# Constant rows at another place, a final norm on VectorE, scratch in a PSUM bank, a priority for SSD

## The chip, the cores and the metric

The kernel runs on one core of a Trainium2 chip. The core has five engines that each work through their own list of instructions in order: TensorE (PE, matmuls), VectorE (DVE), ScalarE (ACT), GpSimd (POOL) and SyncE (SP, which here only issues transfers). TensorE writes to PSUM, a small memory of eight banks per core, and everything else lives in SBUF or in DRAM. The metric is the time of one execution on the device in microseconds, smaller being better; the median of several runs counts.

## The reference

One layer of a hybrid diffusion transformer with 2048 latent tokens and 256 context tokens, width 1024. Three groups of heads share one input projection: pooling, a bidirectional state-space scan (SSD) and a bidirectional gated delta rule (GDN). Then come an output projection, a mixture of 16 experts in which each expert chooses 256 tokens, and a last RMSNorm.

```python
def rms_norm(x, g):
    x32 = x.astype(F32)
    y = x32 * lax.rsqrt(jnp.mean(x32 * x32, axis=-1, keepdims=True) + EPS) * g.astype(F32)
    return y.astype(x.dtype)
...
def gdn_chunked(q, k, v, g, beta, s0):
...
    xm = jnp.where(strict, jnp.einsum('bnhik,bnhjk->bnhij', kb, kc) * decay, 0.0)
    eye = jnp.eye(CHUNK, dtype=xm.dtype)
    tm = lax.linalg.triangular_solve(xm + eye, jnp.broadcast_to(eye, xm.shape), left_side=True, lower=True,
                                     unit_diagonal=True)
    u = jnp.einsum('bnhij,bnhjv->bnhiv', tm, vc * bc[..., None])
    w = jnp.einsum('bnhij,bnhjk->bnhik', tm, kb * jnp.exp(gc)[..., None])
...
def ssd_chunked(xdt, log_a, bm, cm, s0):
...
    states = jnp.einsum('bchjs,bchjp->bchsp', bc * jnp.exp(ac[..., -1:] - ac)[..., None], xc)
    chunk_decay = jnp.exp(ac[..., -1])

    def step(s, inp):
        st, dc = inp
        return s * dc[..., None, None] + st, s
```

The triangular solve is what the inverse in the kernel computes, and the last `rms_norm` is the final norm.

## The kernel before

Precise float32 products are made of three faster ones: a helper `mm3` (lines 133 to 135) multiplies high by high, low by high and high by low parts, and `split` (lines 192 and 193) makes the parts, the high one as a rounded copy on ScalarE and the low one as a difference on VectorE. The program is traced in the order of the code, and a scheduler then puts each engine's instructions into one static order by priorities, which follow the code except where a block asks for a higher one (`tc.high_priority`). Each engine works through its own list and never overtakes.

**Start (0 to 173 us).** SyncE's queue loads the modulation weights (`aw` from `ada_w`), the context and latent rows `xt`, and two slices of the input weights whose products `dt`, `ab` and `z` are needed first. Line 295 rounds such a slice to `wzh`, line 296 makes `wzl`. `raw_T` transposes the normed rows into `raw` (lines 240 to 245), `modulate` scales them (line 350) and splits them into `hTh` and `hTl`, `t1_ctx` (line 371 copies its result into a buffer) and `t1` multiply. Between them lines 334 to 343 write constant rows (ones and minus ones that later scans read as parts of larger rows) into `gpq_d` and `fsr_d` in DRAM, from buffers of `zrow()`: a pool of two buffers named `zt` which also hold the scratch of line 230, the copy of line 371 and the results of `t1`.

**Projection and convolutions (173 to 660 us)** and some preparation (to 780 us) are not touched.

**Scans (780 to 1450 us).** GDN needs for each chunk the inverse of a unit lower triangular matrix. `gdn_inv` does this by columns on blocks of 32: `column(c)` multiplies an outer product into a scratch tile (line 1071) and subtracts it (line 1073), 31 columns for each block, on VectorE. The GDN chain itself goes step by step: line 1163 updates the state `gS` of each direction from a matmul in PSUM, line 1135 makes `gR`, lines 1183 to 1190 the output `oe`, which goes to DRAM as `go_d`. The SSD scan goes tile by tile beside it (`ssd_f`, and the output in lines 892 to 932). In the scans, the eight PSUM banks are `pp` (2), `ps` (3, constant NPS), `pm`, `pc` and `po`. A plan in code hands out pieces of inverse, SSD and preparation per step; GDN's preparation asks for priority HPP, the chain for HPO.

**Output projection and router (1450 to 1710 us).** Line 1390 brings `go` back and transposes it, line 1437 takes the projection's results out of PSUM.

**Experts (1710 to 2374 us).** For each of 16 experts: `slots` compares (`oh`, line 1605) and gathers rows, `up` and `down` multiply, `weights` loads a piece `wr` of 128x1024, rounds it (line 1644) and makes its low part `wl` (line 1647) on VectorE. Line 1672 multiplies the gate's result `sg` once per expert. `down` scatters into `x_d`. From expert 9 the final norm runs beside the experts, as a list of tasks of which `up` takes one at each piece of weights: `norm_all` norms all 16 tiles, and `norm_rows(q)` norms again the rows that expert q changed later. `norm_scale` computes a reciprocal root by Newton steps of small operations on VectorE (lines 109 to 120, helper `rsqrt_bits`, tiles `fr1t` and `fr1y` on one column, `fr2t` and `fr2y` on two), scales the tile on ScalarE (line 1693) and multiplies with `fg` on GpSimd (line 1694). The last three experts write their rows directly, in one product on VectorE (line 1691).

## Time and profile before

| | |
|---|---|
| median of 3 runs | 2382.78 us (2379.66 to 2393.21) |
| the profiled execution, its own time | 2376.19 us |
| span in its profile | 2374.4 us |
| busy: TensorE, VectorE, ScalarE, GpSimd | 2078.8, 1734.5, 1077.7, 826.5 us |
| transferred | 424.72 MB, mean 179 GB/s |

The span is the time between the first and the last instruction of the profiled execution; its own time is that of the whole launch. Busy times are sums over the whole span, and stages differ: an engine that is idle on average can be full in a stage, so that the rows further down are taken stage by stage.

### The profile page before, as it was taken

The numbers are of one execution on the slowest core, as the hardware profiler recorded it, in microseconds if no ns is written. First come the engines' busy times: TensorE is split into PE (matmuls) and PEld (weight loads), VectorE is DVE, ScalarE is ACT, GpSimd is POOL, SyncE is SP. The second block draws the span as 40 slices with busy tenths as digits, with TensorE's granted clock in tenths as the row PEclk, the third lists the DMA queues.
The fourth block names the chain that finished last, engine by engine and source line by source line (L and its number), as shares of the span: only waits on it lengthen the run. The fifth ranks groups of instructions, "written<-read, shape, count | busy, mean of one in ns | idle before, by whom it ended". The sixth has DMA issues, their size and how long they took to land. (4 is left out here: it accounts for less than half of the span.)

```text
span 2374.4 us, 44609 instructions
## 1 busy us (share of the span) xinstructions
PE 2078.8 (88%) x16769; PEld 1793.8 (76%) x16769; DVE 1734.5 (73%) x3638; ACT 1077.7 (45%) x2136; POOL 826.5 (35%) x752
## 2 busy tenths in 40 slices
PE   5789999999989567998997897997599999988886
PEld 2788888888867456787886786885489999987785
DVE  7666776877754698998998865545656766789877
ACT  5443333443315345656655442554144444455552
POOL 2002333355330444553543551443421111124454
PEclk7899999999999778999998899998699999999998
DMA  7533333433323897998886766654368778788893
GB/s 237 122 94 92 87 113 120 133 112 90 94 65 78 225 249 180 219 220 211 206 203 158 176 170 194 213 199 162 125 189 243 212 232 225 224 273 286 294 285 143
DMA packets 418033, 424.72 MB, mean 179 GB/s; under 512 B 151987, under 2 KB 312602, under 8 KB 416794
## 3 DMA queue, kind: packets, MB, share of 16 engines
q1 hardware_dynamic: 398106, 368.33, 53.8%
q0 software_dynamic: 14816, 50.03, 7.9%
q10 hardware_dynamic: 4896, 3.51, 0.5%
q8 instruction: 133, 2.18, 0.4%
q14 instruction: 82, 0.67, 0.1%
HBM read 309.55 MB, written 112.22 MB: 178 GB/s over the span
## 5 line engine op out<-in xcount | busy, mean ns | idle before, releaser
L1644 ACT ACTIVATE wh<-wr 128x1024 fp32r<-128x1024 f32 x192 | 202.3, 1056 | 250.1 <-PE pgate L134 71.8
L461 DVE SCALAR_TENSOR_TENSOR acc<-u,PV,acc 128x512 f32<-128x512 f32 (+1 forms) x320 | 286.0, 943 | 37.9 <-ACT acc L459 20.9
L133 PE MATMUL pj<-hTh,wh 128*128 128x512 f32 (+1 forms) x800 | 307.5, 384 | 5.5 <-ACT wh L192 4.5
L135 PE MATMUL pj<-hTh,wl 128*128 128x512 f32 (+1 forms) x800 | 305.9, 383 | 3.4 <-DVE wl L193 3.4
L134 PE MATMUL pj<-hTl,wh 128*128 128x512 f32 (+1 forms) x800 | 308.5, 386 | 0.0
L1647 DVE TENSOR_TENSOR wl<-wr,wh 128x1024 fp32r<-128x1024 f32 x179 | 227.5, 1278 | 99.3 <-ACT wh L1644 99.2
L133 PEld LDWEIGHTS pj<-hTh,wh 128*128 128x128 f32 x800 | 153.1, 191 | 37.5 <-ACT wh L192 4.9
L135 PEld LDWEIGHTS pj<-hTh,wl 128*128 128x128 f32 x800 | 152.9, 191 | 34.3 <-DVE wl L193 4.2
L134 PEld LDWEIGHTS pj<-hTl,wh 128*128 128x128 f32 x800 | 153.1, 191 | 29.4 <-issue 0.7
L506 POOL TENSOR_TENSOR aw<-aw,sc 128x1024 f32<-128x1024 f32 x32 | 66.3, 2071 | 252.2 <-DMA aw<-in_ada_w_dram 241.5
L134 PE MATMUL pgate<-xel,wh 128*128 128x256 f32 x512 | 151.0, 295 | 2.6 <-DVE xel L193 2.6
L133 PE MATMUL pgate<-xeh,wh 128*128 128x256 f32 x512 | 149.0, 291 | 3.9 <-ACT xeh L192 3.8
L135 PE MATMUL pgate<-xeh,wl 128*128 128x256 f32 x512 | 150.1, 293 | 0.0
L133 PE MATMUL pup<-xeh,wh 128*128 128x256 f32 x512 | 149.1, 291 | 0.0
L135 PE MATMUL pup<-xeh,wl 128*128 128x256 f32 x512 | 147.7, 288 | 0.0
L134 PE MATMUL pup<-xel,wh 128*128 128x256 f32 x512 | 147.4, 288 | 0.0
L1747 POOL DMA_INDIRECT x_d<-ye,idx x30 | 47.9, 1597 | 202.2 <-DVE ye L1741 128.6
L1071 DVE TENSOR_TENSOR tmpb<-Wb,Vb 128x31 f32<-128x31 f32 (+15 forms) x217 | 109.3, 504 | 5.7 <-POOL Vb L1063 1.9
L133 PE MATMUL pdown<-wh,hh 128*128 128x512 f32 x256 | 103.7, 405 | 7.7 <-DVE ye L1741 2.3
L1073 DVE TENSOR_TENSOR Vb<-Vb,tmpb 128x31 f32<-128x31 f32 (+15 forms) x217 | 107.4, 495 | 3.7
L1623 POOL DMA_INDIRECT xe<-h_d,idx x32 | 40.2, 1258 | 187.1 <-PE pup L135 115.1
L133 PEld LDWEIGHTS pgate<-xeh,wh 128*128 128x128 f32 x512 | 101.3, 198 | 5.2 <-ACT xeh L192 4.8
(581 smaller groups left out, 5966.6 us busy)
## 6 DMA issues: line engine op xcount, KB each, us to landing
wr<-in_exp_w_gate_dram SPq DMA_DIRECT2D x64, 512.0 KB
wr<-in_exp_w_up_dram SPq DMA_DIRECT2D x64, 512.0 KB
wr<-in_exp_w_down_dram SPq DMA_DIRECT2D x64, 512.0 KB
aw<-in_ada_w_dram SPq DMA_DIRECT2D x32, 512.0 KB
kv<-kv_d SPq DMA_DIRECT2D x72, 192.0 KB
xb<-xb_d SPq DMA_DIRECT2D x35, 320.0 KB
wr<-in_w_in_dram SPq DMA_DIRECT2D x21, 512.0 KB
aw<-in_ada_w_dram SPq DMA_DIRECT2D x8, 1024.0 KB
```

The lines of the kernel that those rows point to most:

```text
L133: TE.matmul(o, lh, rh, start=start, stop=False, **kw)
L134: TE.matmul(o, lh, rl, start=False, stop=False, **kw)
L135: TE.matmul(o, ll, rh, start=False, stop=stop, **kw)
L461: V.scalar_tensor_tensor(av, u[:, s0 - 2 + i:s0 - 2 + i + w], cw[:, i, cb:cb + 1], av, op0=OP.mult, op1=OP.add)
L506: G.tensor_tensor(w, w, sc2[:, :, 0:1].to_broadcast([P, KT, P]), op=OP.mult)
L1071: V.tensor_tensor(t, W[:, c + 1:, c:c + 1].to_broadcast([P, nr, ncl]), N[:, c:c + 1, :ncl].to_broadcast([P, nr, ncl]), op=OP.mult)
L1073: V.tensor_tensor(N[:, c + 1:, :ncl], N[:, c + 1:, :ncl], t, op=OP.subtract)
L1623: r = G.indirect_dma_start(out=XE[e][h], out_offset=None, in_=h2_d, in_offset=rows_of(e, h))
L1644: S.activation(wh, w, AF.Copy)
L1647: r = e.tensor_tensor(wl, w, wh.bitcast(F32), op=OP.subtract)
L1747: G.indirect_dma_start(out=x2_d, out_offset=rows_of(e, h), in_=ys[h], in_offset=None, compute_op=OP.bypass if late else OP.add)
```

## The change

Five edits:

1. The differences `wzl` of line 296 are made by VectorE instead of GpSimd.
2. The constant rows are written by a function `fixed_rows(i)`, one piece in each of the rounds 3 to 5 of the loop over pairs of tiles, from a tile `cr` with one buffer of its own.
3. The inverse's scratch is a PSUM bank `tm` instead of an SBUF tile, and `ps` has two banks instead of three.
4. SSD's forward tiles (`ssd_f`) are traced with a priority of HPS = 1200.
5. In the final norm each tile is scaled and multiplied in one product on VectorE. `norm_all` handles tiles in pairs, with one reciprocal root for both, and stores them in pairs.

```diff
-            G.tensor_tensor(wl[:, ks, :], w, wh[:, ks, :].bitcast(F32), op=OP.subtract)
+            V.tensor_tensor(wl[:, ks, :], w, wh[:, ks, :].bitcast(F32), op=OP.subtract)
...
-        for dst, n, nr, w, h0, h1 in ((gpq_d, NSTEP, 16, GPQ, 0, 6), (fsr_d, 36, 14, FSR, 0, 3), (fsr_d, 36, 14, FSR, 3, 6)):
-            cr = zrow()[0:16]
...
+        def fixed_rows(i):
+            for dst, n, nr, w, h0, h1 in (((gpq_d, NSTEP, 16, GPQ, 0, 6), (fsr_d, 36, 14, FSR, 0, 3), (fsr_d, 36, 14, FSR, 3, 6))[i],):
+                cr = pool.tile([P, 512], F32, name="cr", bufs=1)[0:16]
...
+            if 3 <= g < 6:
+                fixed_rows(g - 3)
...
-            t = gt_("tmpb", [P, 256])[:, :nr * ncl].rearrange("p (r c) -> p r c", c=ncl)
+            t = bank(pb, "tm", [256], 1)[:, :nr * ncl].rearrange("p (r c) -> p r c", c=ncl)
             V.tensor_tensor(t, W[:, c + 1:, c:c + 1].to_broadcast([P, nr, ncl]),
                             N[:, c:c + 1, :ncl].to_broadcast([P, nr, ncl]), op=OP.mult)
             V.tensor_tensor(N[:, c + 1:, :ncl], N[:, c + 1:, :ncl], t, op=OP.subtract)
...
-            f(t)
+            with tc.high_priority(offset=HPS) if f is ssd_f else nullcontext():
+                f(t)
...
-        for i, x in enumerate(xs):
-            if ys:
-                V.scalar_tensor_tensor(ys[i], x, r[:, i:i + 1], fg, op0=OP.mult, op1=OP.mult)
-            else:
-                S.activation(x, x, AF.Copy, scale=r[:, i:i + 1])
-                G.tensor_tensor(x, x, fg, op=OP.mult)
+        for i, (x, y) in enumerate(zip(xs, ys or xs)):
+            V.scalar_tensor_tensor(y, x, r[:, i:i + 1], fg, op0=OP.mult, op1=OP.mult)
...
+            if t % 2 and t >= 3:
+                for q in (t - 3, t - 2):
+                    SY.dma_start(dap(out, q * P * D, [[D, P], [1, D]]), tiles.pop(q))
             if t < NT:
                 tiles[t] = mt("xn", [P, D], 4)
                 SY.dma_start(tiles[t], dap(x2_d, t * P * D, [[D, P], [1, D]]))
-            if 0 <= t - 1 < NT:
-                ss = lp.tile([P, 1], F32, name="fss", bufs=2)
-                norm_sum(tiles[t - 1], ss)
-                norm_scale([tiles[t - 1]], ss)
...
+            if t % 2 == 0 and t >= 2:
+                ss = lp.tile([P, 2], F32, name="fss2", bufs=2)
+                xs = [tiles[t - 2], tiles[t - 1]]
+                for h, x in enumerate(xs):
+                    norm_sum(x, ss[:, h:h + 1])
+                norm_scale(xs, ss)
```

Since a scheduler sets the order, the edits also move what they don't name. A row below is one instruction: its line, its operation, what it writes and reads, and its shape; equal neighbours stand in one row with their count. The lines of the changed kernel are 1 higher in the early part, and 4 or 5 higher in the later ones.

SyncE's queue at the start, before: the weights and rows that are loaded, and the constant rows (to `gpq_d` and `fsr_d`) behind them.

```order
L293 DMA aw<-in_w_in_dram 128x4x12
L204 DMA xt<-in_x_dram 128x1024
L293 DMA aw<-in_w_in_dram 128x4x24
L204 DMA xt<-in_x_dram 128x1024
L293 DMA aw<-in_w_in_dram 128x4x24
L331 DMA gpq_d<-zt 4x36x128
L331 DMA gpq_d<-zt 12x36x384
L331 DMA fsr_d<-zt 2x36x128
L331 DMA fsr_d<-zt 12x36x384
L204 DMA xt<-in_x_dram 128x1024
L331 DMA fsr_d<-zt 12x36x384
L204 DMA xt<-in_x_dram 128x1024 x11
```

The same queue after the change:

```order
L278 DMA aw<-in_ada_w_dram 128x2048
L332 DMA gpq_d<-cr 4x36x128
L332 DMA gpq_d<-cr 12x36x384
L278 DMA aw<-in_ada_w_dram 128x2048 x2
L205 DMA xt<-in_x_dram 128x1024 x2
L294 DMA aw<-in_w_in_dram 128x4x384
L294 DMA aw<-in_w_in_dram 128x4x12
L294 DMA aw<-in_w_in_dram 128x4x384
L294 DMA aw<-in_w_in_dram 128x4x12
L332 DMA fsr_d<-cr 2x36x128
L332 DMA fsr_d<-cr 12x36x384
L205 DMA xt<-in_x_dram 128x1024 x2
```

The constant rows now stand ahead of the last two `ada_w` loads and of most `xt` loads, and not later, since they have a buffer of their own and wait for nothing that the main work holds.

VectorE's list at the end of the scans, before: `syi_11357` is the last SSD tile's output, `gS` the state of the GDN chain, `oe` its output.

```order
L921 TENSOR_TENSOR syi_11357<-ps,syi_11357 128x384
L111 TENSOR_SCALAR grt<-grt 128x6
L112 TENSOR_TENSOR gry<-gry,grt 128x6
L1190 TENSOR_TENSOR oe_14817<-oe_14817,gry 128x384
L1226 TENSOR_TENSOR fx<-pm,fx 128x512
L926 TENSOR_SCALAR sss<-sss 128x1
L109 TENSOR_TENSOR srt<-sry 128x1
L110 TENSOR_TENSOR srt<-srt,sss 128x1
L1163 TENSOR_TENSOR gS_6224<-gSG,pc 64x384 x2
L111 TENSOR_SCALAR srt<-srt 128x1
L1183 TENSOR_TENSOR oe_14950<-po,oe_14950 128x384
L112 TENSOR_TENSOR sry<-sry,srt 128x1
```

The same place after the change, from the last `oe` on:

```order
L1194 TENSOR_TENSOR oe_15029<-oe_15029,gry 128x384
L112 TENSOR_SCALAR srt<-srt 128x1
L113 TENSOR_TENSOR sry<-sry,srt 128x1
L932 TENSOR_SCALAR sy<-sy,sry 128x384
L863 TENSOR_TENSOR S_10969<-ssg,ps 128x384
L1429 TENSOR_SCALAR jt<-jp 32x16
L1430 TENSOR_SCALAR two<-jt 32x16
L898 TENSOR_TENSOR sE<-sE,sEb 128x768
L903 TENSOR_TENSOR sE<-ps,sE 128x384 x2
L914 TENSOR_TENSOR syi_11357<-ps,s_eB 128x384
L1337 TENSOR_SCALAR jm<-jp 128x128
L1341 MEMSET onesb 128x128
```

The last SSD tile (`S_10969` and `syi_11357`) stood between the last two steps of the chain, and now stands behind the last `oe`, beside the constants of the router (`jm`, `onesb`, `jt`).

VectorE's list while `norm_all` runs beside the experts, before: `fss` is the sum of squares, `fr1y` and `fr1t` the Newton steps on one column.

```order
L119 TENSOR_SCALAR fr1y<-fss 128x1
L1647 TENSOR_TENSOR wl<-wr,wh 128x1024
L120 TENSOR_SCALAR fr1y<-fr1y 128x1
L193 TENSOR_TENSOR xel<-ptr,xeh 128x4x128
L1687 TENSOR_SCALAR fss<-fss 128x1
L109 TENSOR_TENSOR fr1t<-fr1y 128x1
L193 TENSOR_TENSOR xel<-ptr,xeh 128x4x128
L119 TENSOR_SCALAR fr1y<-fss 128x1
L110 TENSOR_TENSOR fr1t<-fr1t,fss 128x1
L1605 TENSOR_SCALAR oh<-iota_s,SL 128x256 x3
L120 TENSOR_SCALAR fr1y<-fr1y 128x1
L111 TENSOR_SCALAR fr1t<-fr1t 128x1
```

After the change, where two tiles have one set of steps on two columns (`fr2y`, `fr2t`) and the products that GpSimd had stand on VectorE:

```order
L121 TENSOR_SCALAR fr2y<-fr2y 128x2
L113 TENSOR_TENSOR fr2y<-fr2y,fr2t 128x2
L110 TENSOR_TENSOR fr2t<-fr2y 128x2
L1695 SCALAR_TENSOR_TENSOR xn<-xn,fr2y,fg 128x1024 x2
L111 TENSOR_TENSOR fr2t<-fr2t,fss_22228 128x2
L1652 TENSOR_TENSOR wl<-wr,wh 128x1024
L112 TENSOR_SCALAR fr2t<-fr2t 128x2
L1652 TENSOR_TENSOR wl<-wr,wh 128x1024
L113 TENSOR_TENSOR fr2y<-fr2y,fr2t 128x2
L1677 TENSOR_TENSOR sg<-sg,pup 128x1024
L110 TENSOR_TENSOR fr2t<-fr2y 128x2
L1652 TENSOR_TENSOR wl<-wr,wh 128x1024
```

The steps are half as many, and two products of 128x1024 follow a set of them. GpSimd's list keeps no instruction of the final norm but the indirect transfers.

## Rows read from the trace of the kernel before

**Rows 1.** Windows of four stages: busy us and instructions of each engine, clock, DMA.

```profile
0.00:38.00 38.00, 24.84 (x96) 9.47 (x97) 26.62 (x56) 23.35 (x23) 4.42 (x13) 0.91 0.92 348
38.00:173.00 135.00, 99.83 (x543) 94.06 (x542) 94.70 (x340) 59.38 (x136) 7.65 (x5) 0.86 0.39 97
...
780.00:1340.00 560.00, 461.34 (x6205) 396.50 (x6205) 492.29 (x984) 302.64 (x885) 253.53 (x274) 0.89 0.85 206
...
2100.00:2220.00 120.00, 103.60 (x723) 92.79 (x722) 114.81 (x305) 70.71 (x89) 48.91 (x23) 0.96 0.82 281
```

**Rows 2.** Timeline, 38 to 73 us: start, us, work, count [idle before <-releaser].

```profile
40.59 8.53 DVE L350 TENSOR_SCALAR raw<-raw,A,B 128x256 f32<-128x256 f32 x5
40.84 7.48 POOL L296 TENSOR_TENSOR wzl<-aw,wzh 128x1680 fp32r<-128x1680 f32 x2 [35.45 <-ACT wzh L295]
50.04 0.43 PE L134 MATMUL pt<-hTl,wzh 128*36 128x256 f32 x1 [8.49 <-DVE hTl L193]
...
62.64 0.54 DVE L341 TENSOR_SCALAR zt<-dsel 16x384 f32<-16x384 f32 x1 [8.59 <-DMA gpq_d<-zt]
63.57 0.43 PE L134 MATMUL pt<-hTl,wzh 128*36 128x256 f32 x1 [6.79 <-DVE hTl L193]
72.00 0.36 ACT L371 COPY zt<-pt 36x256 f32<-36x256 f32 x1 [5.40 <-DMA fsr_d<-zt]
72.41 0.42 PE L374 MATMUL pt<-ident,zt 36*128 36x36 f32 x2 [6.92 <-ACT zt L371]
```

**Rows 3.** The page's groups: work xcount | busy us, mean ns | idle before.

```profile
L1073 DVE TENSOR_TENSOR Vb<-Vb,tmpb 128x31 f32<-128x31 f32 (+15 forms) x217 | 107.4, 495 | 3.7
```

**Rows 4.** Timeline of VectorE and GpSimd, 1042 to 1063 us.

```profile
1042.88 0.42 DVE L1073 TENSOR_TENSOR Vb<-Vb,tmpb 128x252 f32<-128x252 f32 x1
...
1049.13 0.87 POOL L1123 TENSOR_TENSOR ke<-kv,g_kes 128x384 f32<-128x384 f32 x1
1049.34 0.91 DVE L1073 TENSOR_TENSOR Vb<-Vb,tmpb 128x231 f32<-128x231 f32 x1
...
1062.80 0.19 DVE L1073 TENSOR_TENSOR Vb<-Vb,tmpb 128x31 f32<-128x31 f32 x1
```

**Rows 5.** Two lines over the whole trace: count, duration in ns min/median/max, first, last.

```profile
L1163 DVE TENSOR_TENSOR gS<-gSG,pc x68: 533/552/560, 897.8 to 1440.8; 64x384 f32<-64x384 f32 x68
...
L894 DVE TENSOR_TENSOR sE<-sE,sEb x16: 946/958/2570, 930.9 to 1428.4; 128x768 f32<-128x768 f32 x16
```

**Rows 6.** Timeline of VectorE, the chain's step at 1340 us.

```profile
1340.34 1.13 DVE L1163 TENSOR_TENSOR gS<-gSG,pc 64x384 f32<-64x384 f32 x2
```

**Rows 7.** Timeline of VectorE and TensorE, 1442 to 1467 us.

```profile
1442.73 0.52 DVE L928 TENSOR_SCALAR sy<-sy,sry 128x384 f32<-128x384 f32 x1
...
1456.80 0.55 DVE L1190 TENSOR_TENSOR oe<-oe,gry 128x384 f32<-128x384 f32 x1
...
1466.56 0.90 PE L1390 MATMUL ptr<-ident,go 128*128 128x128 f32 x3 [3.08 <-DMA go<-go_d]
```

**Rows 8.** Timeline of VectorE: line 1672 of three experts.

```profile
2022.82 1.22 DVE L1672 TENSOR_TENSOR sg<-sg,pup 128x1024 f32<-128x1024 f32 x1 [0.68 <-PE pup L135]
...
2059.92 1.22 DVE L1672 TENSOR_TENSOR sg<-sg,pup 128x1024 f32<-128x1024 f32 x1 [0.68 <-PE pup L135]
...
2333.65 1.21 DVE L1672 TENSOR_TENSOR sg<-sg,pup 128x1024 f32<-128x1024 f32 x1
```

**Rows 9.** Window 2080:2374, of tile fr1t alone, then of tile fr2t alone (VectorE busy).

```profile
2080.00:2374.00 294.00, 50.29 (x192) 0.92 0.76 257
...
2080.00:2374.00 294.00, 13.79 (x84) 0.92 0.76 257
```

**Rows 10.** Groups of lines, 2080 to 2374 us, columns as in rows 3.

```profile
L1647 DVE TENSOR_TENSOR wl<-wr,wh 128x1024 fp32r<-128x1024 f32 x67 | 91.4, 1368 | 11.0 <-ACT wh L1644 10.9
...
L1694 POOL TENSOR_TENSOR xn<-xn,fg 128x1024 f32<-128x1024 f32 x24 | 61.5, 2612 | 55.6 <-ACT xn L1693 45.9 <-DVE fr1t L109 6.5 <-DMA xn<-x_d,idx 3.1
...
L1691 DVE SCALAR_TENSOR_TENSOR xn<-ye,fr2y,fg 128x1024 f32<-128x1024 f32 x6 | 7.4, 1279 | 0.1
```

More of the change, by code (lines that the diff above doesn't have):

```diff
@@ L45 @@
 HPO = 2000
+HPS = 1200
 NXQ = 2
@@ L50 @@
 NEND = 1
-NPS = 3
+NPS = 2
 HPP = 2000
@@ L332, in put_rows_of @@
                          src[r0:r1, None, :].to_broadcast([r1 - r0, n, src.shape[1]]))
-        for dst, n, nr, w, h0, h1 in ((gpq_d, NSTEP, 16, GPQ, 0, 6), (fsr_d, 36, 14, FSR, 0, 3), (fsr_d, 36, 14, FSR, 3, 6)):
-            cr = zrow()[0:16]
-            if not h0:
-                for d in range(2):
-                    V.tensor_copy(cr[:, 64 * d:64 * d + 64], (dsel[:, 6 + d:7 + d] if nr == 16 else ones[0:16, 0:1])
-                                  .to_broadcast([16, 64]))
-                put_rows_of(dst, cr[:, 0:P], 0, 12, nr, n, nr, w)
-            V.tensor_scalar(cr[:, P:].rearrange("p (h c) -> p h c", h=h1 - h0),
-                            dsel[:, h0:h1, None].to_broadcast([16, h1 - h0, HW // (h1 - h0)]), -1.0, None, op0=OP.mult)
-            put_rows_of(dst, cr[:, P:], P + h0 * P, 0, 12, n, nr, w)
+        def fixed_rows(i):
+            for dst, n, nr, w, h0, h1 in (((gpq_d, NSTEP, 16, GPQ, 0, 6), (fsr_d, 36, 14, FSR, 0, 3), (fsr_d, 36, 14, FSR, 3, 6))[i],):
+                cr = pool.tile([P, 512], F32, name="cr", bufs=1)[0:16]
+                if not h0:
+                    for d in range(2):
+                        V.tensor_copy(cr[:, 64 * d:64 * d + 64], (dsel[:, 6 + d:7 + d] if nr == 16 else ones[0:16, 0:1])
+                                      .to_broadcast([16, 64]))
+                    put_rows_of(dst, cr[:, 0:P], 0, 12, nr, n, nr, w)
+                V.tensor_scalar(cr[:, P:].rearrange("p (h c) -> p h c", h=h1 - h0),
+                                dsel[:, h0:h1, None].to_broadcast([16, h1 - h0, HW // (h1 - h0)]), -1.0, None, op0=OP.mult)
+                put_rows_of(dst, cr[:, P:], P + h0 * P, 0, 12, n, nr, w)
         def modulate(tiles):
@@ L1703, in task @@
                 SY.dma_start(tiles[t], dap(x2_d, t * P * D, [[D, P], [1, D]]))
-            if 0 <= t - 1 < NT:
-                ss = lp.tile([P, 1], F32, name="fss", bufs=2)
-                norm_sum(tiles[t - 1], ss)
-                norm_scale([tiles[t - 1]], ss)
-            if 0 <= t - 2 < NT:
-                SY.dma_start(dap(out, (t - 2) * P * D, [[D, P], [1, D]]), tiles.pop(t - 2))
+            if t % 2 == 0 and t >= 2:
[4 more added lines that the diff above has]
+                norm_scale(xs, ss)
         return [lambda t=t: task(t) for t in range(NT + 2)]
```

## The prediction, made before the result was known

> **What bounds the kernel now.** I read the views in this order: the table of windows to see which engine fills each stage, then the timeline of the stage in which each edit lands, then the groups of the lines that change. [rows 1] gives four stages. From 0 to 38 us the DMA engines are 92% busy at 348 GB/s: loading bounds it. From 38 to 173 us no engine is full (TensorE 100 of 135 us, VectorE 95, DMA 39%), so single waits decide. In the scans, 780 to 1340 us, VectorE is busy 492 of 560 us and TensorE 461: VectorE is closest to full. In 2100 to 2220 us, experts with the final norm beside them, VectorE is busy 114.8 of 120 us and TensorE only 103.6: VectorE bounds.
>
> [rows 8] prices that last stage. The product `sg` comes once per expert. Between 2022.82 and 2059.92 us a step is 37.10 us, and VectorE had waited there for TensorE's `pup`: TensorE sets the pace. From 2059.92 to 2333.65 us, six steps take 273.7 us, 45.6 each, and `sg` waits for nothing. So 273.7 - 6 x 37.1 = 51 us is the most that this stage can give.
>
> **Edit 1: the split of `wz` to VectorE, constant rows on a tile of their own.** [rows 2] is the start. On GpSimd the two differences `wzl` take 7.48 us from 40.84; in the same stretch five 128x256 scalings on VectorE take 8.53 us from 40.59, and the low half `hTl` behind them comes so late that TensorE waits 8.49 us. On VectorE a product of 128x1024 takes 1.28 us [rows 10], so a difference of 1680 columns about 2 us, two of them 4 us. I take a gain of 8.49 - 4 = 4 us there.
>
> Then come two waits on the `zt` buffers, which the constant rows hold while a slow DMA reads them: VectorE's third constant row waits 8.59 us for `gpq_d`, and TensorE behind it 6.79 us for `hTl`; ScalarE's copy waits 5.40 us for `fsr_d`, and TensorE behind it 6.92. With a tile `cr` of its own nothing in the main work waits for these DMAs: -6.8 and -6.9 (or 5.4, if TensorE's other 1.5 us have another cause).
>
> Against it stands the order. The scheduler does not put these DMAs later: on SyncE's queue two of them now stand ahead of the last two `ada_w` loads, one ahead of `x` loads. There the DMA engines are 92% busy, against 39% after 38 us [rows 1]. The waits for them in [rows 2] are 5.40 and 8.59 us, so in the saturated stretch they cost up to some 12 us if most of this comes on top, and nothing if their packets fit between others. I take 6 us. Sum: -4 - 6.8 - 6.9 + 6 = -12; the bounds are -18 (nothing lost to DMA) and 0 (12 lost, and the 8.49 only moves to `wzl`, which VectorE now computes itself).
>
> **Edit 2: the inverse's scratch in PSUM, one `ps` bank fewer, a priority for SSD.** The second operation of a column, line 1073, costs 107.4 us for 217 [rows 3]. Alone it takes 0.19 us for 31 columns and 0.42 for 252 [rows 4]: 1.04 ns a column over a fixed part. A call has 31 columns c of (31-c)(c+1) elements, 176 on average: 0.34 us, and 217 x 0.34 = 74 us. The other 33 us are stretching: in [rows 4] the one of 231 columns takes 0.91 us while GpSimd multiplies `ke`. [rows 5] shows who is stretched: line 1163, with one input in PSUM, stays within 533 to 560 ns over 68 instructions; line 894, with both in SBUF, goes from 946 to 2570. After the change line 1073 reads `tm` from PSUM and is of the first kind: -33 us of VectorE. Line 1071 keeps two SBUF inputs and gains nothing; what its write to PSUM costs no row shows: between 0 and the whole fixed part of the 31-column row again, some 0.16 x 217 = 35 us. I take nothing, because the read of PSUM in line 1163 costs nothing either: 552 ns for 384 columns, against 0.55 us in line 1190 with both inputs in SBUF [rows 7].
>
> [...]
>
> How much of 33 us reaches the end? The GDN chain (line 1163, twice a step) makes 33 steps in 542.5 us, 16.4 each [rows 5]. The seven steps from 1340.34 [rows 6] to the last (its second line 1163 at 1440.8, its first at 1440.3), with no inverse left beside them, still take 14.3 each. So VectorE's load costs the chain some 2.1 us a step, 69 us in all, of which the stretching is a part; VectorE is busy 88% of the stage, and some of its idle time will only grow. I take 20 of the 33.
>
> On the other side, the last forward tile of SSD falls behind: it stood between the last two steps of the chain, and now stands behind the last `oe`. Its work took from 1428.4 us (the last line 894, [rows 5]) to 1442.73 (line 928, [rows 7]): 14.3 us. Before, TensorE waited after the last `oe` (1456.80) until 1466.56 for `go` to come back from memory [rows 7]; 10 us of the tile can hide there if TensorE, which takes things in order, isn't held. The rest, 4 us, and a few for two instead of three `ps` banks: I take +10, from 4 to 40. Sum -10; bounds -33 + 4, say -30, and +35 without any gain on the chain.
>
> **Edit 3: the norm on VectorE, tiles in pairs.** [rows 9]: the small Newton steps on single columns cost 50.3 us for 192, 262 ns each, where those on two columns take 13.8 for 84, 164 ns. Eight pairs need half as many: 96 x 0.164 = 15.8. So -34.5. Added are 24 products of 128x1024, at 1.28 us [rows 10]: +30.7. GpSimd loses its 24 products of 61.5 us, and with them what they stretch: `wl` takes 1368 ns for 67 here, 1.28 at most by the product beside it, so at least 67 x 0.09 = 6. VectorE is left with -34.5 + 30.7 - 6 = -10 us, and ScalarE loses the 24 scalings. More comes from the chain: a product on GpSimd takes 2.6 us, and the indirect transfers of the next expert queue behind them on GpSimd's queue. I take -20, of the 51 that the stage could give; bounds -5 (VectorE stays full, and the stores in pairs hold the weight loads behind them on SyncE) and -45.
>
> **Sum.** -12 - 10 - 20 = -42 on the profiled execution of 2376.2: 2334. The median of the runs shown, 2382.8, is 0.28% above it; scaled so, 2340.
>
> **Rivals.** A, *every stretched microsecond comes back*: the expert step falls to TensorE's 37.1 (-45), the scans keep 25, the start 16. For it: VectorE is the fullest engine in both stages. Against: after the edit VectorE still needs about as long per expert as TensorE, and two engines that are both full don't overlap perfectly. -86: 2297. B, *only the last stage gains*: the constant rows pay in the saturated DMA what they gain in waits, and the SSD tail eats the scan's gain: -20, 2363. For it: the DMA share of 92%; against: the chain's steps, longer with an inverse beside them. C, *slower by the banks*: with two `ps` banks the SSD tiles overlap less. Sixteen tiles [rows 5] of 14.3 us are 229 us of such work; if each is lengthened by half, as two thirds of the banks would make it, that is 115 us, and if half of this holds TensorE ahead of the chain, +57; with the tail's 14 and the 20 gained, +51, less 32 from the other edits: +19, 2402. It decides once the scans lose over 32 us. Against it: TensorE is not full there, and the chain comes first by its own priority.
>
> D, *PSUM costs time at each access*: if the write of line 1071 costs its whole bound of 35 us of VectorE, and 0.6 of that reaches the end as with the 33, it takes 21 of the 42 back: -21, 2362. For it: no row of this trace has VectorE writing to PSUM. Against: reading from there is free [rows 5, 7]. [...]
>
> **How the numbers follow.** Forecast 0.48 (2318 to 2360 is its own range), A 0.16, B 0.17, C 0.10, D 0.09. Half of a percent, 12 us, is about what measurements of this kernel can tell from nothing. Faster by more than that: the forecast, A, D and six tenths of B, 0.83. Within it: the rest of B and the weak end of C, 0.10. Slower: 0.07. The range 2306 to 2372 reaches into A and over nearly all of B and D, and leaves out most of A (0.09) and of C (0.09).
>
> **What would show it.** Right: between 38 and 75 us no wait of TensorE for `hTl` above 3 us, and the transposes behind `zt` (72.41 us before) near 60; line 1073 within 560 ns, line 1071 still stretched; the chain's steps below 16 us; the last line 894 behind the last `oe`; expert steps near 42 us with no GpSimd product. Wrong: `ada_w` loads that end over 10 us later, line 1071 longer than its 0.42 us at 252 columns when nothing runs beside it, `ps` waits on TensorE within the chain, or weight loads that stand behind a store on SyncE in the last stage.

## The result, and the profile after

The changed kernel takes 2359.6 us (median of 4, 2345.3 to 2362.5), against 2384.5 before: a ratio of 0.989, 95% interval 0.987 to 0.992. The forecast was 2340 within 2306 to 2372. The profiled execution is the slowest of the four: 2362.5 us, span 2360.7, 13.7 below the span before. The profiled execution before took 2376.2 us, less than any of its kernel's four runs (2379.7 to 2393.2). So the two profiles show 14 us of the 25 between the medians, and the other 11 stand in no stage below. The views here are of the changed kernel's profiled execution, in which lines are numbered 1 to 5 higher than in [rows 1 to 10].

The table of windows, for the stages of [rows 1] that changed:

```profile
38.00:173.00 135.00, 113.83 (x610) 103.02 (x611) 103.48 (x357) 65.44 (x148) 5.76 (x10) 0.89 0.43 118
780.00:1340.00 560.00, 480.31 (x6724) 411.75 (x6724) 473.15 (x1013) 315.92 (x921) 252.92 (x268) 0.92 0.83 208
2100.00:2220.00 120.00, 112.19 (x830) 103.78 (x828) 98.70 (x239) 62.35 (x79) 25.36 (x16) 0.94 0.92 310
```

VectorE is less busy in the scans (473 against 492 us) and far less among the experts (98.7 of 120 against 114.8). Where did that go? The first and last starts of a few lines cut the span into stretches. All kernels of this study stand in one table, so that the experiments can be read against it (us from the start of the span; "median" is that of the runs, or a single one where marked; a convolution product is VectorE's `acc<-u,PV,acc`, line 461; `sg` comes once per expert):

| kernel | median | first conv. product | last conv. product | SSD's last (928) | chain's last `oe` (1190) | last `xo` (1437) | first `sg` | last `sg` |
|---|---|---|---|---|---|---|---|---|
| before | 2384.5 | 186.0 | 652.0 | 1442.7 | 1456.8 | 1637.8 | 1730.7 | 2333.7 |
| changed | 2359.6 | 170.7 | 637.2 | 1443.2 | 1424.1 | 1623.1 | 1716.2 | 2318.1 |
| own_tile | 2382.2 | 174.3 | 640.9 | 1450.1 | 1464.2 | 1644.9 | 1738.5 | 2342.5 |
| start_only | 2400.9 | 170.3 | 637.9 | 1458.4 | 1461.0 | 1650.2 | 1741.6 | 2349.7 |
| norm_only | 2367.2 | 186.0 | 651.2 | 1450.8 | 1465.2 | 1647.3 | 1739.3 | 2329.3 |
| scratch_only | 2404.0 | 186.3 | 653.6 | 1475.7 | 1439.5 | 1655.2 | 1748.1 | 2356.7 |
| no_hps | 2386.5 | 171.9 | 639.1 | 1473.1 | 1428.4 | 1652.3 | 1745.3 | 2343.9 |
| no_scratch | 2386.1 | 169.8 | 637.5 | 1446.8 | 1471.6 | 1653.5 | 1746.9 | 2341.2 |
| ssd_first | 2347.9 | 170.1 | 639.2 | 1412.4 | 1444.4 | 1625.4 | 1718.5 | 2307.2 |
| ssd_1700 | 2353.0 | 169.7 | 637.3 | 1446.4 | 1430.4 | 1626.1 | 1719.1 | 2308.2 |
| late_spread | 2371.2 | 170.6 | 637.9 | 1442.8 | 1423.4 | 1621.4 | 1714.3 | 2327.4 |
| rows_later | 2349.9 | 168.8 | 637.1 | 1437.7 | 1419.0 | 1617.7 | 1710.9 | 2306.2 |
| after_nostore | 2354.1 (one) | 169.9 | 636.8 | 1437.9 | 1419.6 | 1617.4 | 1710.7 | 2309.8 |
| before_nostore | 2396.2 (one) | 185.6 | 651.9 | 1443.4 | 1457.3 | 1638.2 | 1731.6 | 2351.6 |

From before to changed: 15.3 us are won at the first convolution product and 14.8 at the last. At the output projection's end it is still 14.7, though the chain's last `oe` is 32.7 earlier; at the last `sg` it is 15.6. So the start gave all of it, the scans and the experts next to nothing, in this execution.

The start, TensorE's timeline; the waits of 8.49, 6.79 and 6.92 us of [rows 2] are gone:

```profile
58.06 0.43 PE L134 MATMUL pt<-hTh,wzh 128*36 128x256 f32 x1 [2.03 <-ACT wzh L296]
60.21 0.43 PE L136 MATMUL pt<-hTh,wzl 128*36 128x256 f32 x1 [1.51 <-DVE wzl L297]
65.58 0.43 PE L376 MATMUL pt<-ident,zt 36*128 36x36 f32 x2 [0.46 <-ACT zt L373]
```

The two lines of a column of the inverse as groups (columns as in [rows 3]): the first of them before, then both after, then the second after over the whole trace (columns as in [rows 5]):

```profile
L1071 DVE TENSOR_TENSOR tmpb<-Wb,Vb 128x31 f32<-128x31 f32 (+15 forms) x217 | 109.3, 504 | 5.7 <-POOL Vb L1063 1.9
...
L1075 DVE TENSOR_TENSOR tm<-Wb,Vb 128x31 f32<-128x31 f32 (+15 forms) x217 | 112.8, 520 | 5.6 <-POOL Vb L1067 1.6
L1077 DVE TENSOR_TENSOR Vb<-Vb,tm 128x31 f32<-128x31 f32 (+15 forms) x217 | 72.4, 334 | 3.9
...
L1077 DVE TENSOR_TENSOR Vb<-Vb,tm x217: 169/353/422, 804.4 to 1278.5; 128x31 f32<-128x31 f32 x8, 128x87 f32<-128x87 f32 x8, 128x135 f32<-128x135 f32 x8, 128x175 f32<-128x175 f32 x8
```

The second (line 1073 before) went from 107.4 us [rows 3] to 72.4 and never exceeds 422 ns; the first (line 1071), which writes to PSUM now, went from 109.3 us to 112.8. The four lines that end the scans and the projection, as first and last starts, with the last of them before the change on top:

```profile
L1437 DVE TENSOR_TENSOR xo<-po,xo x32: 679/692/694, 1476.5 to 1637.8; 128x512 f32<-128x512 f32 x32
...
L1167 DVE TENSOR_TENSOR gS<-gSG,pc x68: 531/557/586, 884.6 to 1408.4; 64x384 f32<-64x384 f32 x68
...
L932 DVE TENSOR_SCALAR sy<-sy,sry x16: 401/414/497, 929.9 to 1443.2; 128x384 f32<-128x384 f32 x16
...
L1194 DVE TENSOR_TENSOR oe<-oe,gry x16: 545/557/1148, 1192.6 to 1424.1; 128x384 f32<-128x384 f32 x16
...
L1442 DVE TENSOR_TENSOR xo<-po,xo x32: 679/692/693, 1457.3 to 1623.1; 128x512 f32<-128x512 f32 x32
```

The chain takes 523.8 us in place of 543.0 (its first to its last line 1163), and SSD ends 19 us behind it. The timeline of ScalarE, VectorE and TensorE shows the end of the last SSD tile:

```profile
1438.82 0.19 ACT L929 ACTIVATION_READ_ACCUMULATOR zt<-sy 128x1 f32 x1
...
1440.01 1.22 DVE L1411 SCALAR_TENSOR_TENSOR mrow<-mrow,g2row 128x1024 f32<-128x1024 f32 x1 [4.35 <-DMA g2row<-in_norm_g_dram]
...
1441.50 0.31 DVE L930 TENSOR_SCALAR sss<-sss 128x1 f32<-128x1 f32 x1
...
1443.18 0.42 DVE L932 TENSOR_SCALAR sy<-sy,sry 128x384 f32<-128x384 f32 x1
...
1443.74 0.88 PE L936 MATMUL ps<-ident,sy 128*128 128x128 f32 x3 [9.62 <-DVE sy L932]
```

TensorE waits 9.62 us for the last SSD tile. Some 2.5 us of that are the router's: its `mrow` waits for a row from memory, and SSD's last norm, whose sum ScalarE had finished at 1439.0, stands behind it in VectorE's list and starts at 1441.5. The rest is the tile's own work.

The experts: groups of lines from 2060 us on, and the small steps of tile `fr2t` in that window (there is no `fr1t` any more):

```profile
L1652 DVE TENSOR_TENSOR wl<-wr,wh 128x1024 fp32r<-128x1024 f32 x69 | 84.2, 1221 | 35.4 <-ACT wh L1649 34.4 <-DMA out_dram<-xn 0.9
L1695 DVE SCALAR_TENSOR_TENSOR xn<-xn,fr2y,fg 128x1024 f32<-128x1024 f32 x24 | 29.7, 1281 | 0.3
...
2060.00:2360.00 300.00, 28.87 (x180) 0.91 0.77 256
```

VectorE got what the forecast counted: small steps 28.9 us in place of 50.3 + 13.8 [rows 9], 24 products in 29.7, `wl` 1221 ns in place of 1368 [rows 10]. But `wl` now waits 34 us for ScalarE, in place of 11 [rows 10]. The six steps from the `sg` of expert 9 to that of expert 15 were 47.5, 43.4, 51.2, 42.2, 41.9 and 47.6 us before; they are 42.6, 38.3, 50.4, 40.7, 54.6 and 45.7 now. Five steps won 0.8 to 5.1 us each, 14.2 together, and the fifth of the six lost 12.7. That fifth step, in the timeline of VectorE, ScalarE and TensorE:

```profile
2217.79 1.21 DVE L1677 TENSOR_TENSOR sg<-sg,pup 128x1024 f32<-128x1024 f32 x1
...
2257.19 1.06 ACT L1649 ACTIVATE wh<-wr 128x1024 fp32r<-128x1024 f32 x1 [1.82 <-PE pup L135]
...
2262.75 0.28 PE L136 MATMUL pup<-xeh,wl 128*128 128x256 f32 x1
...
2269.11 1.06 ACT L1689 ACTIVATE fsq<-xn 128x1024 bf16<-128x1024 f32 x1 [10.86 <-DMA xn<-x_d,idx]
...
2270.17 1.04 ACT L1649 ACTIVATE wh<-wr 128x1024 fp32r<-128x1024 f32 x1
...
2271.24 1.22 DVE L1652 TENSOR_TENSOR wl<-wr,wh 128x1024 fp32r<-128x1024 f32 x1 [11.51 <-ACT wh L1649]
2272.38 1.21 DVE L1677 TENSOR_TENSOR sg<-sg,pup 128x1024 f32<-128x1024 f32 x1
...
2275.89 0.77 PE L134 MATMUL pdown<-wh,hh 128*128 128x512 f32 x1 [7.39 <-DVE fr2t L110]
```

ScalarE stands at the square `fsq` of a renormed row for 10.86 us; the next rounding `wh`, hence `wl` on VectorE, hence `sg`, stand behind it. TensorE had ended the last `pup` product that `sg` reads at 2263.0, 9.3 us before `sg` starts, so the weights in question are of a later piece; TensorE then stands still for 7.39 us, until VectorE has gone on. The chain of waits says what the square waited for (start, us, what):

```profile
2246.93 6.33 DMA x_d<-ye,idx
2253.52 9.42 DMA x_d<-ye,idx
2263.20 5.83 DMA xn<-x_d,idx
```

Two scatters of an expert's result and then the gather of the same rows, one after the other: 21.6 us, all of it on the way to a rounding of weights that has nothing to do with them.

### The profile page after: what moved, and what is told of

The parts are those of the page before. It is cut to its first block, busy times and chain, and to the rows that moved or that the text cites. A ratio compares the mean times of both kernels' runs of the same rounds, so it can differ in the third digit from the quotient of the medians.

```text
span 2360.7 us, 44437 instructions
## 1 busy us (share of the span) xinstructions
PE 2082.4 (88%) x16769; PEld 1792.4 (76%) x16769; DVE 1667.6 (71%) x3544; ACT 1056.4 (45%) x2112; POOL 763.7 (32%) x726
## 5 line engine op out<-in xcount | busy, mean ns | idle before, releaser
L1652 DVE TENSOR_TENSOR wl<-wr,wh 128x1024 fp32r<-128x1024 f32 x179 | 217.8, 1222 | 123.7 <-ACT wh L1649 122.7
L1075 DVE TENSOR_TENSOR tm<-Wb,Vb 128x31 f32<-128x31 f32 (+15 forms) x217 | 112.8, 520 | 5.6 <-POOL Vb L1067 1.6
L135 PEld LDWEIGHTS pgate<-xel,wh 128*128 128x128 f32 x512 | 103.1, 201 | 4.9 <-DVE xel L194 4.9
```

Source lines behind the costliest of these rows:

```text
L135: TE.matmul(o, lh, rl, start=False, stop=False, **kw)
L1075: V.tensor_tensor(t, W[:, c + 1:, c:c + 1].to_broadcast([P, nr, ncl]), N[:, c:c + 1, :ncl].to_broadcast([P, nr, ncl]), op=OP.mult)
L1652: r = e.tensor_tensor(wl, w, wh.bitcast(F32), op=OP.subtract)
```

## The experiments

Three theories were to be told apart for each stage. For the start: is it the tile, or the place in the code, and how much is the difference `wzl`? For the scans: why does a chain that is 19 us shorter give nothing? For the experts: did the transfers' volume become the bound, or the order on an engine?

**norm_only**, the kernel before with edit 5 alone (the last two hunks of the diff above).

> The kernel before with edit 5 alone: the final norm on VectorE and in pairs. Theory (DMA): in the changed kernel the DMA engines are 94 to 99% busy in 2080 to 2220 us, and the sixteen sg products take as long from first to last as before (601.9 against 603.0 us), so the norm's freed VectorE time only meets the bound of the transfers: sg from first to last within 5 us of 603, the DMA share of the norm's stretch rises above 0.9, total within 8 us of before. Rival (my forecast): VectorE was the bound and 20 us come back, 2365. Second rival: the edit gains its 20 us alone, and it is the scan's changed order that loses them in the changed kernel; then this one is faster by 12 us or more.

Measured: 2367.2 us, ratio 0.993 (0.991 to 0.996). First to last `sg` 590 us, 13 less than before. The theory of the volume missed: edit 5 is worth some 13 to 17 us alone, and the changed kernel's experts (601.9) lose them again. In this profile the scans took 10 us longer than before, with the same lists on all engines up to the experts: one execution's stretch of the scans is known to no better than that. (TensorE's granted clock from 880 to 1460 us was 0.92 in both executions; what makes the difference isn't shown.)

**start_only**, the kernel before with edits 1 and 2 (their hunks above).

> The kernel before with edits 1 and 2 alone (differences wzl on VectorE, constant rows from a tile of their own in the rounds 3 to 5). Theory: this is the whole gain of the changed kernel, whose first convolution product starts 15.3 us earlier (170.7 against 186.0) and whose end comes 13.7 earlier: total -13 to -16 us, near 2369. Rival (the scans and the norm each give something of their own): less than 10 us here. Rival (constant rows pay in the DMA's full stretch): within 5 us of before.

Measured: 2400.9, ratio 1.008 (1.006 to 1.011): slower. The first convolution product comes 15.7 us earlier, as expected, and the last 14.1; then the scans and the projection take 1012.3 us in place of 985.8. The theory that a gain at the start arrives at the end fell.

**scratch_only**, the kernel before with edit 3.

```diff
-NPS = 3
+NPS = 2
...
-            t = gt_("tmpb", [P, 256])[:, :nr * ncl].rearrange("p (r c) -> p r c", c=ncl)
+            t = bank(pb, "tm", [256], 1)[:, :nr * ncl].rearrange("p (r c) -> p r c", c=ncl)
```

> The kernel before with the scratch in PSUM and two ps banks, without the priority for SSD. Theory: line 1073 stays below 560 ns and the chain of line 1163 ends 15 to 20 us earlier (before: 897.8 to 1440.8 us, 543 us; here some 525), but the last SSD tiles stand behind the chain in VectorE's list, so that the output projection starts no more than 3 us earlier and the total stays within 6 us of before. Rival: VectorE's freed 33 us reach the end, -10 us or more. Rival: two banks hold the SSD tiles and the chain so long that it is slower by over 12 us.

Measured: 2404.0, ratio 1.010 (1.007 to 1.012). The chain is 13.9 us shorter (529.1), line 1073 at most 423 ns, and SSD's last tile 33 us later: the second rival, slower.

**no_hps**, the changed kernel without edit 4.

```diff
-            with tc.high_priority(offset=HPS) if f is ssd_f else nullcontext():
-                f(t)
+            f(t)
```

> The changed kernel without the priority for SSD's forward tiles. In VectorE's list the last three SSD outputs then stand behind the last step of the chain, where the changed kernel has two. Theory: the SSD tail is what gives back the chain's gain; one more tile of it costs some 10 us more: 2368 against 2360. Rival: the tail hides behind other waits, and nothing moves (within 4 us of the changed kernel).

Measured: 2386.5, 1.001 of before (0.999 to 1.003), 27 us above the changed kernel. SSD ends at 1473.1 in place of 1443.2, so the tail is what gives the gain back, at three times the size that I expected. The three lines that end the scans:

```profile
L932 DVE TENSOR_SCALAR sy<-sy,sry x16: 406/416/990, 947.6 to 1473.1; 128x384 f32<-128x384 f32 x16
...
L1194 DVE TENSOR_TENSOR oe<-oe,gry x16: 544/558/1327, 1192.0 to 1428.4; 128x384 f32<-128x384 f32 x16
...
L1442 DVE TENSOR_TENSOR xo<-po,xo x32: 683/692/693, 1487.1 to 1652.3; 128x512 f32<-128x512 f32 x32
```

1473.1 + 179.5 = 1652.6: the projection's end follows SSD, 44.7 us behind the chain. From these six traces came a rule: the last `xo` starts at the later of SSD's last line 928 plus 179.5 and the chain's last 1190 plus 181.

**ssd_first**, the changed kernel with all SSD tiles ahead.

```diff
-HPS = 1200
+HPS = 2000
...
-            with tc.high_priority(offset=HPS) if f is ssd_f else nullcontext():
+            with tc.high_priority(offset=HPS):
```

> The changed kernel with the priority 2000 instead of 1200 and for all SSD tiles, backward ones too. In VectorE's list the last SSD output then stands ahead of the last step of the GDN chain, as in the kernel before. Theory: the output projection ends at the later of two, 179.5 us after the last SSD tile (line 928) and 181 us after the last line 1190, to within 2 us in five of the six traces so far (the sixth, the start alone, is 8 us later); in the changed kernel SSD ends last (1443.2 against 1424.1 for the chain). With SSD ahead the chain sets the end, and the projection ends up to 18 us earlier: total 2342 to 2352. Rival: SSD's work ahead of the chain lengthens the chain by as much (VectorE is full there), total 2355 to 2365.

Measured: 2347.9, ratio 0.986 (0.982 to 0.989): 12 us below the changed kernel, though the runs of the two overlap (2343.6 to 2352.6 and 2345.3 to 2362.5).

```profile
L932 DVE TENSOR_SCALAR sy<-sy,sry x16: 405/414/953, 901.6 to 1412.4; 128x384 f32<-128x384 f32 x16
...
L1194 DVE TENSOR_TENSOR oe<-oe,gry x16: 544/559/2057, 1214.0 to 1444.4; 128x384 f32<-128x384 f32 x16
...
L1442 DVE TENSOR_TENSOR xo<-po,xo x32: 677/691/692, 1464.1 to 1625.4; 128x512 f32<-128x512 f32 x32
```

1444.4 + 181 = 1625.4: the rule held, but the projection's end is 2 us later than in the changed kernel, the same within what one profile tells. The rival was right for the scans: SSD came 31 us forward and pushed the chain back by 20. The gain in the total is the experts' (588.7 us for the `sg`, the fifth step 41.8), because the new order happens to have the squares behind the roundings there: `sg` starts 0.04 us after the end of the last `pup` product, and not 9.3.

**late_spread**, the norm over more experts.

```diff
-LATE = 7
+LATE = 8
...
-                tasks = norm_all()
+                tasks = [f for x in norm_all() for f in [x] + [lambda: None] * 1]
```

> The changed kernel with the final norm begun one expert earlier, and one task of it in every second piece of weights instead of every one; the eighth expert's rows are normed again too, 2 MB more to move. Theory (DMA): the experts' transfers leave a quarter of the DMA engines free until 2046 us and none from 2080 to 2220, so spreading the norm's 16 MB over more experts takes the excess of the last steps (now 272 us for six, where TensorE's own pace gives 223) down: last sg 15 to 30 us earlier, 2330 to 2345. Rival (VectorE's work or the norm's serial chain bounds): the extra expert's norm costs its own time, 2360 to 2375.

Measured: 2371.2, ratio 0.995 (0.993 to 0.998), 12 us above the changed kernel; `sg` first to last 613 us. The step to expert 9 already takes 43.8 us, and none of the others falls below 43.8. The volume theory missed again.

**after_nostore** and **before_nostore**, without the stores of `norm_all`.

```diff
                 for q in (t - 3, t - 2):
-                    SY.dma_start(dap(out, q * P * D, [[D, P], [1, D]]), tiles.pop(q))
+                    tiles.pop(q)
```

> The changed kernel without the sixteen stores of the normed tiles (their rows of the output stay unwritten unless an expert writes them): 8.4 MB less to move in the experts 10 to 12. Theory (DMA): at some 310 GB/s that is 27 us of transfers, the first-to-last time of sg falls from 602 by 15 to 27 us. Rival (VectorE): its work is the same, under 5 us.

> The kernel before without the same sixteen stores. Theory: before, VectorE and the transfers were both near full in that stretch (VectorE 95.7%, DMA 82% busy in 2100 to 2220 us), so the same 8.4 MB give less than in the changed kernel: 0 to 10 us from the 603 of first to last sg. Rival (the transfers already bounded the kernel before): 15 us or more.

Measured, one run each: 2354.1 and 2396.2; `sg` first to last 599.1 (601.9 with the stores) and 620.0 (603.0 with them). The transfers of 2000 to 2340 us in the changed kernel, then without the stores:

```profile
DMA packets 34384, 87.64 MB, mean 258 GB/s; under 512 B 2665, under 2 KB 2665, under 8 KB 34355
```

```profile
DMA packets 31775, 79.16 MB, mean 233 GB/s; under 512 B 2400, under 2 KB 2400, under 8 KB 31748
```

8.5 MB less are moved, and the steps together take 3 us less where the theory had 15 to 27; in the kernel before they even take 17 us longer. In the changed kernel the DMA share falls from 0.79 to 0.75 over this window, and between 2102 and 2221 us the engines move 247 GB/s in place of 307. Without the stores the scheduler also put the experts' work in another order in both kernels, so this test isn't clean; the next one keeps the volume and moves the order.

**rows_later**, the changed kernel with the squares of expert 12's renormed rows behind the next expert's weights. Its stores of these rows come behind expert 13's, so that rows which both chose keep the older value. The squares of the experts 9 to 11 go back by one task too, and each square gets an order behind the last rounding traced ahead of it (a part of the edit that is left out below).

```diff
+DELAY = 8
...
-                    tasks.append(lambda q=q: norm_rows(q))
+                    rest = {}
+                    tasks.append(lambda q=q, r=rest: r.update(f=norm_rows(q)))
+                    later.append((len(tasks) - 1 + (DELAY if q == NE - DIRECT - 1 else 1), rest))
```

> The changed kernel with one thing moved: the two squares of expert 12's renormed rows (with their scaling and stores) stand in ScalarE's list behind the weights of the next expert, and no longer between two roundings of expert 14's weights. The volume that is moved, VectorE's work and the lists up to there are the same. Theory (in-order ScalarE): in the changed kernel one of these squares waits 10.86 us for a gather that itself waits for two scatters, with a rounding wh behind it, and the step to expert 14's sg takes 54.6 us (55.6 without SSD's priority, same order), where it takes 41.8 and 45.3 in the two kernels whose order has the squares behind seven roundings. Here it takes 42 to 46, and the total is 2345 to 2352, 8 to 14 us below the changed kernel. Rival (the transfers' volume bounds these steps): the step stays above 50 and the total within 4 us of 2360; the same if the gathers only come late for the steps behind.

Measured: 2349.9, ratio 0.985 (0.982 to 0.989). The fifth step takes 45.7 us in place of 54.6, as expected, and `sg` waits for TensorE again:

```profile
2256.45 0.28 PE L137 MATMUL pup<-xeh,wl 128*128 128x256 f32 x1
...
2256.77 1.22 DVE L1684 TENSOR_TENSOR sg<-sg,pup 128x1024 f32<-128x1024 f32 x1 [0.63 <-PE pup L137]
```

The sixth step takes 49.4 in place of 45.7, and the four ahead of the fifth 1.5 less together, so that `sg` from first to last is 6.6 us shorter (595.3). The rest of the total's 10 us is the scans' (5 us in this profile, in which nothing was changed there). The place of the squares on ScalarE sets the fifth step, at the same volume of transfers.

**no_scratch**, the changed kernel without edit 3 (its two lines above, reversed).

> The changed kernel without edit 3: the inverse's scratch is in SBUF again and ps has three banks; the other edits and the priority 1200 for SSD stay. Theory (edit 3 buys nothing in the end): line 1073 is stretched again, but the SSD tiles overlap better with three banks; the stretch from the end of the convolutions to the end of the output projection takes 986 us within 4 (985.8 before, 985.9 in the changed kernel, 986.2 with SSD first), total within 6 us of the changed kernel when the last six expert steps are taken out. Rival (the 33 us of stretching that edit 3 removes are worth 10 us or more on the chain): that stretch takes 996 or more. Rival (the third bank is worth more than the scratch): 980 or less.

Measured: 2386.1, 1.002 of before (1.000 to 1.004); the fifth expert step takes 54.3 us, with the squares ahead of the roundings again. The stretch from the last convolution product to the last `xo` takes 1016 us, 30 more than in the changed kernel: my theory fell, the first rival holds (line 1073 takes up to 2297 ns again). The chain takes 558.8 us and ends last (1471.6 + 181 = 1652.6; 1653.5 measured), SSD would have allowed 1626.3.

**own_tile**, the kernel before with a tile of its own for the constant rows, at the old place.

```diff
-            cr = zrow()[0:16]
+            cr = pool.tile([P, 512], F32, name="cr", bufs=1)[0:16]
```

> The kernel before with one thing changed: the constant rows get a tile of their own and stay where they stand in the code. SyncE's list then has the same head as in the changed kernel, constant rows ahead of the last two ada_w loads. Theory: the tile is all of edit 2, and the place in the code does nothing. The modulation's matmuls end 5 us later than before (39.8 against 34.5 us), and still the first convolution product starts 9 to 13 us earlier than 186.0, the difference to the 15.3 of the changed kernel being edit 1. Rival (the place in the loop matters): under 5 us. The total says little of this, since the scheduler's order of the scans changes with it: with the start alone that cost some 26 us; here it may come out anywhere from 2365 to 2405.

Measured: 2382.2, 1.000 of before (0.998 to 1.002). The first convolution product comes 11.7 us earlier, within the 9 to 13 that were expected of the tile alone. The modulation's last product starts at 42.8 us in place of 35.9 (the 34.5 and 39.8 of the expectation are of its high half; that one starts at 41.0 here). What is left to edit 1 stands in TensorE's timeline:

```profile
61.98 0.43 PE L135 MATMUL pt<-hTh,wzl 128*36 128x256 f32 x1 [3.21 <-POOL wzl L296]
65.96 0.43 PE L135 MATMUL pt<-hTh,wzl 128*36 128x256 f32 x1 [1.21 <-POOL wzl L296]
69.60 0.43 PE L374 MATMUL pt<-ident,zt 36*128 36x36 f32 x2 [0.96 <-ACT zt L371]
```

Two waits for GpSimd's `wzl`, 4.4 us together; in start_only, with edit 1 and the new place in the code, the first product comes 4.0 us earlier still, which leaves about nothing to the place. And again the scans lose what the start gained: 1004 us in place of 985.8.

**ssd_1700**, between the changed kernel and ssd_first.

```diff
-HPS = 2000
+HPS = 1700
```

> The changed kernel with priority 1700 for all SSD tiles, between its 1200 for the forward ones and the 2000 for all that gave 2348. The last SSD tile stands behind the chain's last output again, the one before ahead of it. Expert 14's weights are rounded ahead of the squares of renormed rows. Theory: the projection ends at the later of SSD's end + 179.5 us and the chain's last 1190 + 181; here the two should be nearer to each other than in either kernel, 1612 to 1623 for the projection's end, and six expert steps of 255 to 262 us in place of 272; total 2335 to 2348. Rival (VectorE's work in the scans fixes the end whatever the order): projection ends at 1623 to 1626 and only the experts gain, 2346 to 2352.

Measured: 2353.0, ratio 0.987 (0.983 to 0.991). SSD's 1446.4 + 179.5 = 1625.9, measured 1626.1; the chain would have allowed 1611.4. Six expert steps take 259.7 us. The rival holds to within 1 us: no gain in the scans over the changed kernel, only among the experts. Of the versions that write the whole output, ssd_first has the lowest median of the study.

## Why the prediction was right, and where not

The time lay in the range and the direction was right. The sum was too large: of its 42 us, 14 showed in the profiled spans and 25 in the medians. The number alone doesn't speak for the forecast, since 2359.6 lies nearer to rival B's 2363 and D's 2362 than to 2340. Neither is borne out as a whole: D fell (below), and of B the SSD tail came true, while the start, which it put at nothing, gave all of the profiled gain. C's mechanism is there too, in scratch_only, where SSD ends 33 us later; edit 4 takes it back. (The prediction's Edit 1 is the edits 1 and 2 of the list, its Edit 2 the edits 3 and 4, its Edit 3 edit 5.)

Of the signs, these came true: no wait of TensorE for `hTl` at the start, line 1073 at most 422 ns, line 1071 still stretched, chain steps of 523.8 / 33 = 15.9 us, the last line 894 behind the last `oe`. Two did not: the transposes behind `zt` start at 65.58 us and not near 60, and the expert steps run from 38.3 to 54.6 us and not near 42.

**Start, forecast -12, measured -15.** Edit 1 was sized right (4 us; start_only against own_tile 4.0). The price of the constant rows in the full DMA stretch was forecast 6 us; the modulation's last product starts 6.6 us later (35.9 to 42.5). By the transposes behind `zt` only 6.8 us are won (72.41 to 65.58), less than the sum's 12; the other 8.5 come behind them, from a term that the sum did not have. The eleven `xt` loads queued behind the third constant row on SyncE began at 64.36 us and begin at 56.06 now. Before, ScalarE waited 7.21 us for the first of them:

```profile
81.89 1.06 ACT L230 ACTIVATE zt<-xt 128x1024 bf16<-128x1024 f32 x1 [7.21 <-DMA xt<-in_x_dram]
```

In the changed kernel that square of `xt` starts at 66.48 us and waits for nothing. That the total of -15 lies near -12 is in part luck: the 5 us by which the sum was too large up to the transposes and the 8.5 that it left out behind them have opposite signs.

**Scans, forecast -10, measured 0 in the profiled executions.** With the same lists up to the experts, the stretch from the last convolution product to the last `xo` took 985.8, 986.3 and 996.1 us before (before, before_nostore, norm_only) and 985.9, 980.6, 980.6 and 983.5 after (changed, rows_later, after_nostore, late_spread): on average 989 and 983, so -7, in the range of -30 to +35 and near the sum's term, though single executions differ by 10. VectorE's part was right (33 us forecast, 35 measured at line 1073). The chain's (20 forecast, 19.2 measured) is right by luck: it is the difference of two larger terms. With the start's edits in, edit 3 shortens the chain by 29.8 us (start_only to no_hps, 563.8 to 534.0) or 35.0 (no_scratch to changed, 558.8 to 523.8), about all of the stretching (alone it gave 13.9, in scratch_only), and the start's edits had lengthened it by 20.8 (543.0 to 563.8). The term that was mis-sized is the tail, "+10, from 4 to 40", which measured 18: I let 10 of its 14.3 us hide in the wait for `go`. They did not, as the 9.62 us wait of TensorE shows, and the projection's end follows SSD, 18 us after what the chain would allow. In fourteen traces the rule of the later of two holds within 1.1 us in thirteen; why start_only is 8 us later is open. So edits 3 and 4 are worth nothing one by one, and 26 to 30 us together, once edits 1 and 2 are in: without 4 SSD ends last at 1652, without 3 the chain ends last at 1653, with both it is 1623.

There was a term that the sum did not have: what the start's edits cost the scans. own_tile and start_only changed nothing in the scans' code and lengthened them to 1004 and 1012 us, 15 and 23 above the three executions' average. The scheduler's lists came out otherwise in all of the scans; which of the many moved instructions costs this is open. Edits 3 and 4 make it up, which is why their 26 to 30 us leave only some 7 against the kernel before.

Rival D fell: line 1071's write to PSUM costs (112.8 - 109.3) / 217 = 16 ns on average, 3.5 us in all and not 35. At equal shapes and with no GpSimd instruction beside it, it is 6 ns (the mean over the shapes of both traces). The read from PSUM costs nothing that shows: with 176 columns on average and a PSUM input line 1077 takes 334 ns, and the price worked out from SBUF inputs alone [rows 4] was 340. These 334 ns are the mean both of the operations beside a GpSimd instruction and of those without one; before, the two means were 742 and 333. With one SBUF input it is no longer stretched (at most 422 ns); line 1075 keeps two and is still stretched (up to 1767 ns).

**Experts, forecast -20, measured -1 in the profiled execution.** Five of the six steps became shorter, as forecast. Over the kernels of this study with the same tasks, the `sg` take 594 us on average in six traces with edit 5 (589 to 602) and 606 in four without it (603 to 609): -12. The step that failed is "more comes from the chain": the serial chain of scatters and gathers stayed, GpSimd without products merely issued it at other times, and ScalarE's list put its end ahead of weights. With the same late code the fifth step takes 54.6, 55.6 and 54.3 us where the squares of expert 12's rows stand between its roundings (changed, no_hps, no_scratch), and 41.8, 45.3 and 47.3 where they stand behind them (ssd_first, norm_only, ssd_1700). In the first three `sg` starts 9.3, 9.9 and 8.8 us after the end of the last `pup` product, in the other three at most 0.2. rows_later moved little else, and got 45.7. Why the third of the six steps still takes 46 to 50 us in all of these is open.

## What to carry to other kernels

Where a scheduler makes one static order of everything, an edit in one stage can cost in another that it doesn't touch: time the stages apart, by the first and last start of the same lines, and try edits together before dropping one, since with two chains that end near each other each alone leaves the other last. In an engine's in-order list look for the instruction that waits on a slow transfer and ask what stands behind it: here a square held ScalarE for 10.86 us, with a rounding behind it, although GpSimd had been freed of its 24 products. A high DMA share did not show that the volume was the limit: the DMA engines were 91% busy in the fifth expert step (2218 to 2272 us), and rows_later took 9 us off its 54.6 at the same volume.

## What the runs showed of the hardware that was not expected

VectorE writes a product of SBUF operands to PSUM at nearly the price of a write to SBUF: 520 against 504 ns on average, both stretched beside GpSimd instructions (652 and 759 ns, against 350 and 336 without one), and 6 ns more at equal shapes without GpSimd. Leaving out 8.5 MB of 87.6 between 2000 and 2340 us, where the DMA engines are 79% busy (92% from 2100 to 2220), changed the time from the first to the last `sg` by 3 us of 602, in one run and with another order. The same lists of instructions differ by up to 10 us of 990 between executions of the scans and the projection, while the experts whose pace TensorE sets repeat at 37.09 to 37.11 us.
